# Packing four rows a partition into one slot, with larger store pieces in two half stores, in a transfer-bound SwiGLU kernel

## Chip, cores, metric

One core of a Trainium2 chip. Kernels are compared only within the same rounds. The metric is the device time of one execution in microseconds; lower is better. A "piece" below is one contiguous run of bytes in one partition that a transfer moves; in these traces each piece is one DMA packet.

## The reference

```python
x: float32 [8192, 8192]
a, b = np.split(x, 2, axis=-1)
return a * (b / (1 + np.exp(-b)))        # float32 [8192, 4096]
```

268 MB go in, 134 MB come out; nothing is read twice. The arithmetic is one SiLU and one product for each output element.

## The kernel before

Three slots of 64 KiB in each partition take turns. A slot gets two rows of x a partition (one load of 128 pieces of 64 KiB, 8 MiB). ScalarE overwrites b with SiLU(b), VectorE writes the product over the first half of the slot, and a store of 128 pieces of 32 KiB (4 MiB) sends it out. Loads are issued by SyncE (SP), stores by ScalarE's queue, so they are in two DMA queues (q1 and q10 in the profile).

```python
R = 2; BUFS = 3
xv = x.tensor.reshape([N // R, R * M]).ap()          # one partition line: 2 rows, 64 KiB
ov = out.tensor.reshape([N // R, R * half]).ap()     # one partition line: 2 rows, 32 KiB
...
def swiglu(i, k, c0=0, cw=half):
    xt = tiles[i]
    b = xt[:, k * M + half + c0 : k * M + half + c0 + cw]
    nc.scalar.activation(out=b, in_=b, func=_SILU)
    nc.vector.tensor_mul(out=xt[:, k * half + c0 : ...], in0=xt[:, k * M + c0 : ...], in1=b)
...
for i in range(BUFS):
    load(i)
for i in range(last):
    for k in range(R):
        swiglu(i, k)
    ...
    store(i)
    nxt = i + BUFS
    if nxt < last:
        load(nxt)            # waits until the store of the same slot has landed
    ...                      # the last tile is loaded and stored in smaller parts
```

Of the kernel before, what the change touches and what calls it, by code (L numbers as in the profile page):

```python
# [1 line left out]

# [4 lines left out]

_SILU = mybir.ActivationFunctionType.Silu


@with_exitstack
def kernel(
    ctx: ExitStack,
    tc: tile.TileContext,
    x: bass.AP,
    out: bass.AP,
):




    nc = tc.nc
    N, M = x.shape
    half = M // 2
    P = nc.NUM_PARTITIONS
    R = 2
    BUFS = 3

    xv = x.tensor.reshape([N // R, R * M]).ap()  # L30
    ov = out.tensor.reshape([N // R, R * half]).ap()
    ntiles = N // (P * R)
    last = ntiles - 1

    pool = ctx.enter_context(tc.tile_pool(name="sbuf", bufs=BUFS))
    ctx.enter_context(tc.manual_schedule())
    tiles = {}

    def load(i, rows=None):
        if i not in tiles:  # L40
            tiles[i] = pool.tile([P, R * M], x.dtype, name="xt")
        lo, hi = (0, R) if rows is None else rows
        nc.sync.dma_start(  # L43
            out=tiles[i][:, lo * M : hi * M], in_=xv[i * P : (i + 1) * P, lo * M : hi * M]
        )

    def swiglu(i, k, c0=0, cw=half):
        xt = tiles[i]
        b = xt[:, k * M + half + c0 : k * M + half + c0 + cw]
        nc.scalar.activation(out=b, in_=b, func=_SILU)  # L50
        nc.vector.tensor_mul(  # L51
            out=xt[:, k * half + c0 : k * half + c0 + cw],
            in0=xt[:, k * M + c0 : k * M + c0 + cw],
            in1=b,
        )

    def store(i, c0=0, cw=R * half):
        (nc.scalar if i < last - 1 else nc.sync).dma_start(
            out=ov[i * P : (i + 1) * P, c0 : c0 + cw], in_=tiles[i][:, c0 : c0 + cw]
        )  # L60

    for i in range(BUFS):
        load(i)
    for i in range(last):
        for k in range(R):
            swiglu(i, k)
        if i == last - 1:
            swiglu(last, 0)
        store(i)
        nxt = i + BUFS  # L70
        if nxt < last:
            load(nxt)
        elif nxt == last:
            load(last, (0, 1))
            load(last, (1, 2))

    store(last, 0, half)
    for c0 in range(0, half, half // 2):
        swiglu(last, 1, c0, half // 2)
    store(last, half, half)  # L80


# [1 line left out]
_INS = ['x']  # L84
_OUTS = [((8192, 4096), 'float32')]


# [23 lines left out]
```

## Time and profile before

| | before |
|---|---|
| median, 3 runs before the prediction | 936.1 us (935.9 to 936.24) |
| span of the profiled execution | 934.8 us |
| VectorE, ScalarE busy | 283.3 us, 229.4 us |
| load queue q1, store queue q10, share of the 16 DMA engines | 68.6%, 31.2% |
| bytes moved | 402.65 MB (read 268.44, written 134.22) |

The two queue shares add up to practically all the time of the 16 DMA engines; that is the reading on which everything else stands. The prediction below shows the lines. One view is the order of instructions in the steady part (start, duration, engine and line, what it does; the bracket tells the idle time before it and what ended that):

```profile
398.13 8.95 DVE L51 TENSOR_TENSOR xt<-xt 128x4096 f32<-128x4096 f32 x2 [20.02 <-ACT xt L50]
407.12 0.34 ACTq L58 DMA_DIRECT2D out_dram<-xt  x1
417.89 29.40 SPq L43 DMA_DIRECT2D xt<-in_x_dram  x2
423.51 7.12 ACT L50 ACTIVATE xt<-xt 128x4096 f32<-128x4096 f32 x2 [21.90 <-DMA xt<-in_x_dram]
427.15 8.95 DVE L51 TENSOR_TENSOR xt<-xt 128x4096 f32<-128x4096 f32 x2 [20.07 <-ACT xt L50]
436.14 0.34 ACTq L58 DMA_DIRECT2D out_dram<-xt  x1
```

A store is issued every 29.0 us (407.12, 436.14), and VectorE idles 20 us of them. A store needs 39.7 us to land and a load 34.5, both longer than that distance, so a store is always queued, and so is a load. In the steady part neither queue runs empty.

### The profile page before, as it was taken

How to read it: one execution, taken by the hardware profiler on the slowest of the kernel's cores; microseconds unless marked ns; L12 is line 12 of the kernel's file. 1: busy time of each engine (PE TensorE's matmuls, PEld its weight loads, DVE VectorE, ACT ScalarE, POOL GpSimd, SP SyncE). 2: the span in 40 equal slices, each digit the busy share in tenths (PEclk: the TensorE clock that was granted, in tenths of full speed). 3: DMA queues.
4: the chain of work that ended last, by engine and by line, in shares of the span. 5: the costliest groups of instructions: out<-in, count | busy, mean ns of one | idle time of the engine just before them, and what ended most of it. 6: DMA issues, size and time to landing. Idle time of an engine off the chain costs nothing.

```text
span 934.8 us, 367 instructions
## 1 busy us (share of the span) xinstructions
DVE 283.3 (30%) x65; ACT 229.4 (25%) x66; POOL 0.2 (0%) x4
## 2 busy tenths in 40 slices
DVE  0333312333123331133321333213332133331242
ACT  0223320233302333113331133311333203332041
POOL 0000000000000000000000000000000000000000
DMA  9999999999999999999999999999999999999998
GB/s 404 400 445 430 430 439 433 428 435 443 428 430 439 429 442 432 435 426 453 419 430 452 411 452 423 428 447 425 433 433 453 414 443 429 426 447 428 425 437 376
DMA packets 9506, 402.67 MB, mean 431 GB/s; under 512 B 1056, under 2 KB 1056, under 8 KB 1056
## 3 DMA queue, kind: packets, MB, share of 16 engines
q1 hardware_dynamic: 5184, 276.83, 68.6%
q10 hardware_dynamic: 4320, 125.83, 31.2%
q14 instruction: 2, 0.02, 0.0%
HBM read 268.44 MB, written 134.22 MB: 431 GB/s over the span
## 4 chain that ended last, share of the span: by engine, by line
DMA 84%; DVE 10%; ACT 4%; DVEq 0%; issue 0%; SPq 0%; ACTq 0%
DMA out_dram<-xt 42%; DMA xt<-in_x_dram 42%; DVE xt L51 10%; ACT xt L50 4%; DVEq L106 0%; SPq L43 0%; ACTq L50 0%; DVEq L51 0%
## 5 line engine op out<-in xcount | busy, mean ns | idle before, releaser
L51 DVE TENSOR_TENSOR xt<-xt 128x4096 f32<-128x4096 f32 (+1 forms) x65 | 283.3, 4359 | 637.7 <-ACT xt L50 634.5
L50 ACT ACTIVATE xt<-xt 128x4096 f32<-128x4096 f32 (+1 forms) x65 | 228.1, 3556 | 688.1 <-DMA xt<-in_x_dram 688.1
L50 ACT ACT_TABLE_LOAD x1 | 1.3, 1283 | 0.7 <-PEq L95 0.7
L95 POOL MEMSET const-bfloat16-1.0<- 128x1 bf16 x1 | 0.1, 103 | 0.0
L95 POOL MEMSET const-uint8-127<- 128x1 uint8 x1 | 0.1, 102 | 0.0
L95 POOL MEMSET const-float32-0.0<- 128x1 f32 x1 | 0.1, 100 | 0.2 <-issue 0.2
L95 POOL MEMSET const-float32-1.0<- 128x1 f32 x1 | 0.1, 99 | 0.0
## 6 DMA issues: line engine op xcount, KB each, us to landing
out_dram<-xt ACTq DMA_DIRECT2D x30, 4096.0 KB, 39.7
xt<-in_x_dram SPq DMA_DIRECT2D x2, 4096.0 KB, 27.1
out_dram<-xt SPq DMA_DIRECT2D x1, 4096.0 KB, 23.6
out_dram<-xt SPq DMA_DIRECT2D x2, 2048.0 KB, 14.5
xt<-in_x_dram SPq DMA_DIRECT2D x31, 34.5
```

The source lines that it names most:

```text
L50: nc.scalar.activation(out=b, in_=b, func=_SILU)
L51: nc.vector.tensor_mul(out=xt[:, k * half + c0 : k * half + c0 + cw], in0=xt[:, k * M + c0 : k * M + c0 + cw], in1=b,)
L95: nc = _bacc.Bacc("TRN2", target_bir_lowering=False, num_devices=1)
```

## The change

Its intent: the store's pieces should be 64 KiB too. For that, four rows a partition form a group. Two rows are loaded into a "pack" slot, the other two into an "extra" slot; all four products are written into the pack slot, which is then 64 KiB of finished output. There are two pack slots and one extra slot, so SBUF holds the same 192 KiB a partition. The store goes out in two halves, even and odd partitions, and the next load of the extra slot is made to wait for the first half ("behind"), although the slot is free as soon as VectorE has read it.

```diff
-    R = 2
-    BUFS = 3
+    ngroups = N // (4 * P) - 1
...
+    extra = pool.tile([P, 2 * M], x.dtype, name="extra")
+    packs = [pool.tile([P, 2 * M], x.dtype, name=f"pack{s}") for s in range(2)]
...
+    load_pack(0)
+    load_extra(0)
+    load_pack(1)
+    for g in range(ngroups):
+        pack = packs[g % 2]
+        for k in range(2):
+            swiglu(pack, k, pack, k)
+        for k in range(2):
+            swiglu(extra, k, pack, 2 + k)
+        rows = o4[g * P : (g + 1) * P, :]
+        first = nc.scalar.dma_start(out=rows[0:P:2, :], in_=pack[0:P:2, :])
+        nc.scalar.dma_start(out=rows[1:P:2, :], in_=pack[1:P:2, :])
+        load_extra(g + 1, behind=first)
+        if g + 2 <= ngroups:
+            load_pack(g + 2)
```

(cut: the loads' addresses, and the last 256 x 2 rows, which go through the same half loads and the same three stores from SP as before)

More of the change, by code (lines that the diff above doesn't have):

```diff
@@ L26 @@
     P = nc.NUM_PARTITIONS
-    R = 2
-    BUFS = 3
-    xv = x.tensor.reshape([N // R, R * M]).ap()
-    ov = out.tensor.reshape([N // R, R * half]).ap()
-    ntiles = N // (P * R)
-    last = ntiles - 1
-    pool = ctx.enter_context(tc.tile_pool(name="sbuf", bufs=BUFS))
-    ctx.enter_context(tc.manual_schedule())
-    tiles = {}
-    def load(i, rows=None):
-        if i not in tiles:
-            tiles[i] = pool.tile([P, R * M], x.dtype, name="xt")
-        lo, hi = (0, R) if rows is None else rows
-        nc.sync.dma_start(
-            out=tiles[i][:, lo * M : hi * M], in_=xv[i * P : (i + 1) * P, lo * M : hi * M]
-        )
@@ L47, in swiglu @@
-    def swiglu(i, k, c0=0, cw=half):
-        xt = tiles[i]
-        b = xt[:, k * M + half + c0 : k * M + half + c0 + cw]
+    ngroups = N // (4 * P) - 1
+    sync_dep = mybir.DependencyInfo(mybir.DependencyClass.Sync, mybir.DependencyReason.DATA)
+    x4 = x.tensor.reshape([N // 4, 4 * M]).ap()
+    o4 = out.tensor.reshape([N // 4, 4 * half]).ap()
+    x2 = x.tensor.reshape([N // 2, 2 * M]).ap()
+    o2 = out.tensor.reshape([N // 2, 2 * half]).ap()
+    pool = ctx.enter_context(tc.tile_pool(name="sbuf", bufs=1))
@@ L50, in swiglu @@
+    ctx.enter_context(tc.manual_schedule())
+    extra = pool.tile([P, 2 * M], x.dtype, name="extra")
+    packs = [pool.tile([P, 2 * M], x.dtype, name=f"pack{s}") for s in range(2)]
+    def swiglu(src, k, dst, d, c0=0, cw=half):
+        b = src[:, k * M + half + c0 : k * M + half + c0 + cw]
         nc.scalar.activation(out=b, in_=b, func=_SILU)
         nc.vector.tensor_mul(
-            out=xt[:, k * half + c0 : k * half + c0 + cw],
-            in0=xt[:, k * M + c0 : k * M + c0 + cw],
+            out=dst[:, d * half + c0 : d * half + c0 + cw],
+            in0=src[:, k * M + c0 : k * M + c0 + cw],
@@ L54, in swiglu @@
             in1=b,
         )
-    def store(i, c0=0, cw=R * half):
-        (nc.scalar if i < last - 1 else nc.sync).dma_start(
-            out=ov[i * P : (i + 1) * P, c0 : c0 + cw], in_=tiles[i][:, c0 : c0 + cw]
-        )
-    for i in range(BUFS):
-        load(i)
-    for i in range(last):
-        for k in range(R):
-            swiglu(i, k)
-        if i == last - 1:
-            swiglu(last, 0)
-        store(i)
-        nxt = i + BUFS
-        if nxt < last:
-            load(nxt)
-        elif nxt == last:
-            load(last, (0, 1))
-            load(last, (1, 2))
@@ L77, with load_pack, load_extra @@
-    store(last, 0, half)
+    def load_pack(g):
+        if g < ngroups:
+            src = x4[g * P : (g + 1) * P, : 2 * M]
+        else:
+            src = x2[2 * ngroups * P : (2 * ngroups + 1) * P, :]
+        nc.sync.dma_start(out=packs[g % 2], in_=src)
+    def load_extra(g, behind=None):
+        if g < ngroups:
+            insts = [nc.sync.dma_start(out=extra, in_=x4[g * P : (g + 1) * P, 2 * M :])]
+        else:
+            r0 = (2 * ngroups + 1) * P
+            insts = [
+                nc.sync.dma_start(
+                    out=extra[:, k * M : (k + 1) * M], in_=x2[r0 : r0 + P, k * M : (k + 1) * M]
+                )
+                for k in range(2)
+            ]
+        if behind is not None:
+            tc.add_manual_dep(
+                insts[0].ins, behind.ins.name, sync_dep, reason="half of the store goes first"
+            )
@@ L78 @@
+    pack = packs[ngroups % 2]
+    r0 = 2 * ngroups * P
+    for k in range(2):
+        swiglu(pack, k, pack, k)
+    swiglu(extra, 0, extra, 0)
+    nc.sync.dma_start(out=o2[r0 : r0 + P, :], in_=pack[:, :M])
+    r0 += P
+    nc.sync.dma_start(out=o2[r0 : r0 + P, :half], in_=extra[:, :half])
     for c0 in range(0, half, half // 2):
-        swiglu(last, 1, c0, half // 2)
-    store(last, half, half)
+        swiglu(extra, 1, extra, 1, c0, half // 2)
+    nc.sync.dma_start(out=o2[r0 : r0 + P, half:], in_=extra[:, half:M])
```

## The prediction

> **What bounds the kernel now.** I read the page's first two parts first, to see whether an engine or the transfers are full; then the queues, to count packets; then the windows and the chain, to see whether transfers ever wait for compute.
>
> ```profile
> DVE 283.3 (30%) x65; ACT 229.4 (25%) x66; POOL 0.2 (0%) x4
> ...
> DMA  9999999999999999999999999999999999999998
> ...
> q1 hardware_dynamic: 5184, 276.83, 68.6%
> q10 hardware_dynamic: 4320, 125.83, 31.2%
> ...
> HBM read 268.44 MB, written 134.22 MB: 431 GB/s over the span
> ```
>
> No compute engine is busy for a third of the span; the 16 DMA engines are at 9 tenths or more in 39 of 40 slices. The two queues' shares add up to 99.8% of all engine time (68.6 + 31.2). The reader should see that there is almost nothing to hide better: no byte goes away in this change, so only time per byte, or the 0.2%, can shrink. The windows say the same for the steady part and for the two ends:
>
> ```profile
> 0.00:46.00 46.00, 8.85 (x2) 8.40 (x3) 0.20 (x4) 1.00 0.98 407
> ...
> 59.00:146.00 87.00, 26.48 (x7) 21.37 (x6) 0.00 (x0) 1.00 1.00 434
> 146.00:233.00 87.00, 26.54 (x7) 21.37 (x6) 0.00 (x0) 1.00 1.00 434
> ...
> 900.00:935.00 35.00, 9.51 (x4) 7.33 (x3) 0.00 (x0) 1.00 0.91 393
> ```
>
> The last two columns are the DMA share and GB/s. In the middle the share is 1.00 at 434 GB/s; only the start and the last microseconds are below. The chain of what ended last looks different at first sight:
>
> ```profile
> DMA 84%; DVE 10%; ACT 4%; DVEq 0%; issue 0%; SPq 0%; ACTq 0%
> DMA out_dram<-xt 42%; DMA xt<-in_x_dram 42%; DVE xt L51 10%; ACT xt L50 4%; DVEq L106 0%; SPq L43 0%; ACTq L50 0%; DVEq L51 0%
> ```
>
> It puts 14% on ACT and DVE, because a slot's own cycle is load, compute, store. While one slot computes, the other two keep both queues full, so those 14% are not a gain to be had.
>
> I also read the trace's single packet records. Every data packet is one contiguous piece of one partition, and its duration depends on size alone: 16 KiB 0.611 us, 32 KiB 1.213 us, 64 KiB 2.418 us (medians; in the steady part nearly all equal them), and a completion packet 0.009 us. A straight line through these is 0.602 us per 16 KiB plus about 0.009 us a packet. Summed and divided by 16 engines they give 932.5 us; the first packet starts at 1.7 us and the last ends at 933.6 us. **Work of the DMA engines is the time.**
>
> [...] 65,536 B in 2.418 us is 27.1 GB/s an engine, 433.7 for 16, and the windows show 434. [...] where both queues have work, each 64 KiB load packet is followed by one 32 KiB store packet. [...]
>
> **The change part by part.**
>
> *Store pieces.* Now 30 stores on ACT's queue move 128 pieces of 32 KiB: 8 an engine, 240 in all, 240 x 1.213 = 291.1 us of each engine. After, 15 groups with two halves of 64 pieces of 64 KiB: 4 an engine, 30 x 4 x 2.418 = 290.2 us. Gain **1.0 us**. This is the whole direct saving: a piece costs 0.009 us beyond its bytes, and 120 pieces an engine go away.
>
> *Loads.* 31 full loads and two half loads before and after, with the same piece sizes: 0 us. Completion packets: 33 + 33 transfers before, 33 + 33 after: 0 us.
>
> *Compute.* The same 65 ACTIVATE (3.60 us) and 65 products (4.43 us), only another destination slot: 0 us, and beside transfers in any case.
>
> *Last tiles.* The same half loads, the same three stores from SP (one of 4 MiB, two of 2 MiB): 0 us. The final load still lands some 20 us of transfers before the end, with stores queued, so compute stays covered.
>
> *New waits.* The order has to be played through, since 3 slots now hold a group and a half. Per group an engine has 16 load pieces (38.7 us) and 8 store pieces (19.3 us): 58.0 us. Let the stores be issued at T with R us of the next pack load still to come. Pieces alternate one to one and are equally long, so the pack load ends at T + 2R, the first half store (9.7 us) at T + R + 9.7. The extra load may then start; I allow 1.2 us for the store's completion (last packet's end to the end of the span, 933.6 to 934.8) and 1.3 us for issue (first load: issued 0.73, first packet 1.74). During these 2.5 us the second half store runs alone; its remaining 7.2 us share with the extra load and take 14.3. The extra load then runs its last 12.1 us alone, with the next pack load queued behind it. It lands 1.3 us later, and its two rows need 3.6 + 2 x 4.43 us and small gaps, 12.7 in all, during which the pack load runs. So R = 19.3 - 14.0 = 5.3 us, and the group takes 5.3 + 9.7 + 2.5 + 14.3 + 12.1 + 14.0 = 58 us, which is the work. **No engine idles**: the margin is 7.2 us at the first wait (second half still to send) and 5.3 us at the second (pack load still in the queue). Waiting for the first half thus costs nothing, if half stores run at full rate.
>
> Sum: 936.1 - 1.0 = 935.1 us. Start and end losses (first packet 1.7 us, last receipt 1.2 us, slow first packets) stay.
>
> **Rivals.**
>
> [...] Full collision adds 290 us (1225 us); a quarter of the store time colliding adds 73 us (1008 us). It is the only way that I see to a large loss.
>
> *B, a new bubble.* If the completion of a half store took 10 us instead of 1.2, the extra load would start late and both queues would be empty: 15 x some 2 us, 965 us. Against: in the last part of the trace receipt is 1.2 us, and the margins are 5 us and more.
>
> [...]
>
> *D, faster than the count.* Equal pieces in both queues change how reads and writes mix. Against: load pieces take 2.418 us alone (first 30 us) and beside stores alike; there is nothing to win from another mix. [...]
>
> **Range and chances.** With no collision and no bubble the count is tight: 933 to 937 us. I give this nearly 80%. A gets most of the rest, and spreads from 950 to over 1100 us. The range 932 to 960 takes the first case and a mild form of B or C. Faster by over 2%: 0.01; within 2%: 0.79; slower: 0.20.
>
> **What would show it.** Right: 15 x 2 stores of 64 pieces on ACT's queue, 30 x (64 + 16) = 2400 packets in q10 where 4320 were, at about 31.1% of the span; q1 unchanged in packets; DMA share 1.00 and 434 GB/s in windows of 58 us; half stores 10 to 30 us from issue to landing. Wrong by A: q10's share well above 31%, store packets over 2.418 us, GB/s below 420 in the steady part with the DMA share still near 1. Wrong by B: DMA share below 0.97 in the steady windows with packets at 2.418 us. Wrong by C: load packets longer as well.

The text names two rivals. A: the engines that move a half store of 64 partitions slow each other, so that a store packet takes up to 4.8 us in place of 2.4. That doubling was the author's guess (no transfer in the trace of before had 64 partitions); its 290 and 73 us are estimates from it and from the 290.2 us that the stores take. C: the doubled pitch of the rows slows packets by 1%, also a guess. Two readings that the prediction gives without a count: of the 2308 load packets of 64 KiB between 200 and 800 us that are followed by a data packet, 2303 are followed by one of a store, and of the 3683 between 50 and 900 us, 3666 lie within 1 ns of 2.418 us.

## The result, and the profile after

936.78 us median (936.38 to 937.82, 6 runs) against 936.29 us (935.9 to 937.33, 6 runs) of the kernel before in the same rounds. The ratio is 1.0005, interval 0.9992 to 1.0018: the same. (All ratios are the mean time of one kernel's fast runs over the mean of the other's of the same rounds, so not quite the ratio of the medians.)

The page of the changed kernel, engines, DMA share by slice, queues and the chain of what ended last:

```profile
DVE 281.9 (30%) x65; ACT 229.4 (25%) x66; POOL 0.2 (0%) x4
...
DMA  9999999999999999999999999999999999999998
...
q1 hardware_dynamic: 5184, 276.83, 68.6%
q10 hardware_dynamic: 2400, 125.83, 31.1%
...
HBM read 268.44 MB, written 134.22 MB: 431 GB/s over the span
...
DMA 77%; DVE 14%; ACT 6%; issue 1%; DVEq 0%; SPq 0%; ACTq 0%
```

The store queue has 2400 packets where it had 4320, and its share of engine time went from 31.2% to 31.1%. Half the data packets (1920 in place of 3840), practically the same time: to this resolution a packet's time is its bytes. The windows (us, VectorE and ScalarE busy, GpSimd, clock, DMA share, GB/s):

```profile
0.00:46.00 46.00, 9.31 (x3) 12.51 (x5) 0.20 (x4) 1.00 0.98 416
...
116.00:174.00 58.00, 17.61 (x4) 14.24 (x4) 0.00 (x0) 1.00 1.00 434
174.00:232.00 58.00, 17.61 (x4) 14.24 (x4) 0.00 (x0) 1.00 1.01 434
...
900.00:935.00 35.00, 8.92 (x3) 7.33 (x3) 0.00 (x0) 1.00 0.91 390
```

434 GB/s at full share in the steady part, as before. The order of one group:

```profile
404.39 0.48 ACTq L86 DMA_DIRECT2D out_dram<-pack  x1
404.90 5.21 ACTq L87 DMA_DIRECT2D out_dram<-pack  x1
416.13 7.12 ACT L44 ACTIVATE pack<-pack 128x4096 f32<-128x4096 f32 x2 [17.06 <-DMA pack<-in_x_dram]
419.78 8.95 DVE L45 TENSOR_TENSOR pack<-pack 128x4096 f32<-128x4096 f32 x2 [15.42 <-ACT pack L44]
420.96 0.33 SPq L62 DMA_DIRECT2D extra<-in_x_dram  x1
437.78 0.33 SPq L57 DMA_DIRECT2D pack<-in_x_dram  x1
449.91 7.12 ACT L44 ACTIVATE extra<-extra 128x4096 f32<-128x4096 f32 x2 [26.66 <-DMA extra<-in_x_dram]
453.56 8.76 DVE L45 TENSOR_TENSOR pack<-extra 128x4096 f32<-128x4096 f32 x2 [24.83 <-ACT extra L44]
462.35 0.48 ACTq L86 DMA_DIRECT2D out_dram<-pack  x1
```

The stores go out at T = 404.39, the extra load at T + 16.6, the pack load at T + 33.4, and the next stores at T + 58.0. The prediction's play-through gives 16.2, 33.0 and 58. The chain of what ended last shifts some of its shares from transfers to engines (DMA 84% to 77%, VectorE 10% to 14%, ScalarE 4% to 6%), and the time didn't move. That fits the prediction's reading of the chain: its engine shares aren't time to be gained while another slot's transfers fill the same microseconds.

The trace's packet records (not a view of the page: every packet with its queue, start, duration and size) say where each microsecond is. I use two sums over them, each divided by 16 engines: **stretch**, the time of data packets beyond the usual duration of their size (2.418 us for 64 KiB, 1.213 for 32, 0.611 for 16), and **idle**, the time from the first packet's start to the last packet's end less all packet time. Idle can be slightly negative, because the records of one engine's successive packets overlap by some nanoseconds. A **completion packet** is one of 4 bytes that each engine sends when its share of a transfer is done; the 66 transfers of either kernel left 16 of them each. The records don't name the engine; where the text speaks of one engine, its packets are put together by one ending where the next begins.

| run | median, us | before in its rounds | ratio (95%) | stretch, us | idle, us |
|---|---|---|---|---|---|
| before | 936.29 | | | 2.2 | -0.6 |
| the change | 936.78 | 936.29 | 1.0005 (0.9992 to 1.0018) | 2.6 | -0.3 |
| after_again | 936.61 | 936.32 | 1.0003 (0.9991 to 1.0016) | 2.8 | -0.2 |
| store_blocks | 1160.40 | 936.33 | 1.2387 (1.2366 to 1.2408) | 221.6 | 4.8 |
| load_blocks | 1240.48 | 936.33 | 1.3246 (1.3222 to 1.3270) | 306.4 | -0.6 |
| quarter_pieces | 944.21 | 936.33 | 1.0080 (1.0065 to 1.0095) | | |
| whole_wait | 991.57 | 936.32 | 1.0591 (1.0577 to 1.0606) | 29.7 | 27.8 |
| whole_free | 966.93 | 936.32 | 1.0341 (1.0321 to 1.0362) | 28.0 | 4.8 |
| halves_free | 1010.34 | 936.32 | 1.0791 (1.0776 to 1.0805) | 50.1 | 26.2 |
| quarters_third | 940.48 | 936.11 | 1.0052 (1.0037 to 1.0067) | 7.7 | 0.2 |
| quarters_first | 983.69 | 936.11 | 1.0504 (1.0486 to 1.0521) | 31.0 | 19.3 |
| halves_free_32k | 960.45 | 936.21 | 1.0266 (1.0245 to 1.0286) | 23.5 | 2.4 |
| quarters_first_32k | 940.68 | 936.21 | 1.0046 (1.0030 to 1.0063) | 5.8 | 0.1 |

All outputs are right. The two columns explain the times: for halves_free, 50.1 + 26.2 less the 2.2 - 0.6 of the kernel before is 74.7 us, and it was 74.0 us slower than that kernel. The columns are those of the profiled run, which for quarters_third was its slowest (942.15 us). quarter_pieces has none, since its 8 KiB pieces have no usual duration above. At a threshold of 2%, quarter_pieces, quarters_third and quarters_first_32k count as the same as before, but their intervals lie clear of 1.

### The profile page after: what moved, and what is told of

Read it like the earlier page. It is cut to its first block, busy times and chain, and to the rows that moved or that the text cites. A ratio compares the mean times of both kernels' runs of the same rounds, so it can differ in the third digit from the quotient of the medians.

```text
span 934.6 us, 367 instructions
## 1 busy us (share of the span) xinstructions
DVE 281.9 (30%) x65; ACT 229.4 (25%) x66; POOL 0.2 (0%) x4
## 3 DMA queue, kind: packets, MB, share of 16 engines
q1 hardware_dynamic: 5184, 276.83, 68.6%
q10 hardware_dynamic: 2400, 125.83, 31.1%
## 4 chain that ended last, share of the span: by engine, by line
DMA 77%; DVE 14%; ACT 6%; issue 1%; DVEq 0%; SPq 0%; ACTq 0%
DMA extra<-in_x_dram 51%; DMA out_dram<-pack 27%; DVE pack L45 13%; ACT extra L44 6%; DVE extra L45 0%; DVEq L128 0%; SPq L62 0%; SPq L57 0%; SPq L66 0%; ACTq L44 0%
## 5 line engine op out<-in xcount | busy, mean ns | idle before, releaser
L45 DVE TENSOR_TENSOR pack<-extra 128x4096 f32<-128x4096 f32 x30 | 131.4, 4422 | 359.4 <-ACT extra L44 359.4
L45 DVE TENSOR_TENSOR pack<-pack 128x4096 f32<-128x4096 f32 x32 | 141.6, 4425 | 260.2 <-ACT pack L44 258.5
L44 ACT ACTIVATE extra<-extra 128x4096 f32<-128x4096 f32 (+1 forms) x33 | 114.2, 3505 | 410.5 <-DMA extra<-in_x_dram 410.5
L44 ACT ACTIVATE pack<-pack 128x4096 f32<-128x4096 f32 x32 | 114.0, 3608 | 277.5 <-DMA pack<-in_x_dram 277.5
L45 DVE TENSOR_TENSOR extra<-extra 128x2048 f32<-128x2048 f32 (+1 forms) x3 | 8.9, 3000 | 19.3 <-ACT extra L44 19.3
```

Source lines behind the costliest of these rows:

```text
L45: nc.vector.tensor_mul(out=dst[:, d * half + c0 : d * half + c0 + cw], in0=src[:, k * M + c0 : k * M + c0 + cw], in1=b,)
```

## Experiments

The prediction was right, so the questions are why nothing was lost, where the expected 1 us went, and which parts of the change carry weight. Theory: the DMA engines are full before and after (932.4 and 931.9 us of packet time); the split into even and odd partitions keeps the store packets at 2.418 us, where blocks of 64 neighbouring partitions would not; and the wait for the first half keeps both queues from running empty. Rivals: neither matters; or they matter and for other reasons.

### after_again: is there a microsecond?

No edit; the changed kernel in five more rounds.

> The changed kernel once more, unedited, with more rounds, to size a difference of less than 1 us. Theory of the prediction (each store piece costs about 0.009 us beyond its bytes, 120 fewer per engine): 1.0 us faster than before, ratio 0.999. Theory formed after the result: the records of successive packets overlap by some nanoseconds (waves of load packets start 2.414 us apart but are recorded as 2.418), and the group period fell by only 0.02 us (58.04 to 58.02 us), so the true saving is about 0.3 us, ratio 0.9997, not to be told from 1.

Measured: ratio 1.0003, 0.9991 to 1.0016, again not below 1. The gain of 1.0 us (ratio 0.999) lies just outside both intervals; the 0.9997 of the theory formed after the result lies inside. The records do show the saving in the stores, 291.1 to 290.2 us, but the stretch of load packets took back 0.4 us, and the records overlap less. One stretch of 0.44 us is at 192 to 197 us in both profiles of the changed kernel and not in that of before; I don't know its cause.

### quarter_pieces: what does a packet cost?

The kernel before with the same bytes and waits in four times as many packets:

```diff
-        nc.sync.dma_start(
-            out=tiles[i][:, lo * M : hi * M], in_=xv[i * P : (i + 1) * P, lo * M : hi * M]
-        )
+        for c in range(lo * M, hi * M, M // 2):
+            nc.sync.dma_start(
+                out=tiles[i][:, c : c + M // 2], in_=xv[i * P : (i + 1) * P, c : c + M // 2]
+            )
...
+        step = cw // 4 if i < last - 1 else cw
+        for c in range(c0, c0 + cw, step):     # the store in `step` columns at a time
```

> The kernel before with every load piece cut from 64 to 16 KiB and every steady store piece from 32 to 8 KiB, same ratio of the two, same slots and waits: 1480 more data packets and 185 more completion packets per engine. Theory of the prediction (0.009 us a packet): 1480 x 0.0087 + 185 x 0.009 = 14.5 us more, 951 us. Theory formed after the result (packet records overlap; the true cost of a piece is 2 to 5 ns): 4 to 9 us more, 940 to 945 us. If pieces cost nothing: 936 us.

Measured: 944.21 against 936.33, 7.9 us more for 1480 data and 185 completion packets on each engine: 4.7 ns a packet. The recorded durations sum to 13.1 us more (945.5 against 932.4); successive packets overlap by the rest. If every packet costs the same, the 120 pieces that the change saves are worth about 120 x 4.7 ns = 0.6 us (an estimate), not 1.0, and 0.4 us came back as stretch. The kernel before agrees: on one engine a 32 KiB packet is followed by the next after 1.209 us, a 64 KiB packet after 2.414, so two of the one cost 0.004 us more than one of the other.

### store_blocks and load_blocks: does it matter which 64 partitions?

In store_blocks the halves are partitions 0 to 63 and 64 to 127; in load_blocks the stores stay even and odd, and each extra load of a group is cut at partition 64, both parts behind the first half store. The theory under test is that a block of 64 neighbouring partitions slows the packets, to as much as double their time.

```diff
-        first = nc.scalar.dma_start(out=rows[0:P:2, :], in_=pack[0:P:2, :])
-        nc.scalar.dma_start(out=rows[1:P:2, :], in_=pack[1:P:2, :])
+        first = nc.scalar.dma_start(out=rows[: P // 2, :], in_=pack[: P // 2, :])
+        nc.scalar.dma_start(out=rows[P // 2 :, :], in_=pack[P // 2 :, :])
```

```diff
-            insts = [nc.sync.dma_start(out=extra, in_=x4[g * P : (g + 1) * P, 2 * M :])]
+            src = x4[g * P : (g + 1) * P, 2 * M :]
+            insts = [
+                nc.sync.dma_start(out=extra[h : h + P // 2, :], in_=src[h : h + P // 2, :])
+                for h in (0, P // 2)
+            ]
```

> The two half stores take partitions 0 to 63 and 64 to 127 instead of even and odd ones; waits as in the changed kernel. [...] store packets go from 2.418 us to as much as 4.8 us where all engines are in step, which adds up to 290 us; 1000 to 1225 us, DMA share near 1, load packets still 2.418. Rival (reads from SBUF don't collide, or the share is spread in another way): 936 us, packets unchanged; then the choice of every second partition had no effect and my rival A was no danger in the first place.

> The stores stay even and odd; the 15 extra loads are cut in two transfers of partitions 0 to 63 and 64 to 127, both behind the first half store. Tests writes into SBUF as store_blocks tests reads. [...] these load packets (120 per engine, 290 us) take up to 4.8 us, 1000 to 1225 us. Rival (only reads collide): 936 us; rival (neither collides): 936 us here and in store_blocks.

Queues of store_blocks (packets, MB, share of the 16 engines) and GB/s in 40 slices of the span:

```profile
GB/s 403 430 269 378 371 285 434 260 382 373 274 434 269 376 378 260 434 290 367 392 253 434 281 364 391 260 434 281 357 394 249 434 294 346 403 240 434 305 311 374
...
q1 hardware_dynamic: 5184, 276.83, 56.9%
q10 hardware_dynamic: 2400, 125.83, 42.5%
```

The same 2400 packets and bytes as in the changed kernel now take 42.5% of a longer span, 492 us of each engine in place of 290. The reader should see the slices: 434 GB/s where only loads run, 240 to 300 where stores take most of the slice. In the records the median store packet takes 4.90 us in place of 2.42. Of the 221.6 us of stretch 201.5 lie in store packets; load packets have the other 20, which the expectation had at zero.

Queues of load_blocks:

```profile
q1 hardware_dynamic: 5424, 276.83, 76.1%
q10 hardware_dynamic: 2400, 125.83, 23.7%
```

Here the load queue takes 76.1% of 1238.5 us, 942 us in place of 641, and the median store packet stays at 2.418 us. Over the 120 packets of an engine's extra loads those 301 us are 2.5 us each, so about 4.9 us a packet (an estimate from the two shares). Both runs show that a block of 64 partitions is slow, for stores out of SBUF and for loads into it, and refute the rivals, which all expected 936 us. What in the hardware makes it slow isn't shown. DMA share stays near 1 (0.99 to 1.02 in three windows of store_blocks, at 319 to 363 GB/s, and 9 tenths or more in 39 of 40 slices of load_blocks): the share counts the time that packets take, whatever they move in it. A cause on the DRAM side was not tested by a run of its own, but is unlikely: the whole store of whole_free writes the same contiguous rows, and the whole extra load reads the same rows at the same pitch, both with a median of 2.418 us. In the changed kernel, with even and odd partitions, no packet showed this (store packets at 2.418 us, stretch of all stores 0.06 us). It isn't so in every order of transfers: halves_free and halves_free_32k below, with the same split, have 5.1 and 7.1 us of stretch in store packets, of open cause. How the 64 partitions were dealt to the engines isn't recorded; all that is shown is that this split kept full rate in the changed kernel and the block split did not.

### whole_wait, whole_free, halves_free: what do the halves and the wait do?

whole_wait: one store of all partitions, extra load behind it. whole_free: one store, extra load free of it. halves_free: two halves, extra load free of them.

```diff
-        first = nc.scalar.dma_start(out=rows[0:P:2, :], in_=pack[0:P:2, :])     # whole_wait, whole_free
-        nc.scalar.dma_start(out=rows[1:P:2, :], in_=pack[1:P:2, :])
+        first = nc.scalar.dma_start(out=rows, in_=pack)
...
-        load_extra(g + 1, behind=first)                                          # whole_free, halves_free
+        load_extra(g + 1)
```

> One whole store, and the extra load waits for all of it. Theory: the pack load ends, the store runs alone to its end, then nothing is queued until its completion is seen and the next load issued: 2.2 to 2.5 us idle for all engines per group, 15 x 2.2 to 2.5 = 33 to 37 us, so 969 to 973 us, with the DMA share in steady windows at about 0.96 and packets still 2.418 us. Rival (transfers are covered whatever the order, because the queues are deep): 936 us.

> One store of 128 pieces of 64 KiB in place of two halves, and the extra load doesn't wait for it. Theory: the halves serve only the wait; without it one whole store does as well, 936 us, same as halves_free to 1 us. Rival (halves give something of their own, for example earlier landing): slower by 1% or more than halves_free.

> The wait of the extra load on the first half store is taken away; the extra load then waits only for the products that read its slot. Played through with the prediction's method: extra load and store share from the start, the store ends 38.7 us after its issue, the next pack load is issued 2.5 us later while the load queue still has 2.8 us of work, so no engine idles: 936 us, same within 1 us, with half stores taking longer to land (around 20 us and 40 us in place of 16.5 and 33) and the pack load issued some 41 us after the stores instead of 33. Rival (the wait is what keeps the queues full): a bubble each group, 15 x 1 to 3 us, 950 to 980 us.

All three were slower than expected, halves_free and whole_free against my theory. The order in whole_wait:

```profile
424.71 0.34 ACTq L86 DMA_DIRECT2D out_dram<-pack  x1
437.36 7.12 ACT L44 ACTIVATE pack<-pack 128x4096 f32<-128x4096 f32 x2 [17.97 <-DMA pack<-in_x_dram]
...
452.27 0.33 SPq L62 DMA_DIRECT2D extra<-in_x_dram  x1
452.64 0.43 SPq L57 DMA_DIRECT2D pack<-in_x_dram  x1
473.95 7.12 ACT L44 ACTIVATE extra<-extra 128x4096 f32<-128x4096 f32 x2 [29.46 <-DMA extra<-in_x_dram]
477.60 8.76 DVE L45 TENSOR_TENSOR pack<-extra 128x4096 f32<-128x4096 f32 x2 [27.63 <-ACT extra L44]
486.39 0.34 ACTq L86 DMA_DIRECT2D out_dram<-pack  x1
```

The group takes 61.7 us in place of 58.0. Nothing is queued between the end of the store and the load issued at 452.27, and the records have a gap (fewer than 8 of 16 engines at work) of 1.7 to 2.0 us there in each of the 15 groups. That much was expected. The other half of the loss was not: after each gap the first load packets take 3.1 us (0.65 us an engine), and when the next store starts, each engine's load packet before it takes 3.6 us (1.2 us). The kernel before has this pattern once, at its start (0.6 us) and at its first store (1.5 us).

The order in halves_free:

```profile
434.58 0.33 SPq L62 DMA_DIRECT2D extra<-in_x_dram  x1
434.59 0.48 ACTq L86 DMA_DIRECT2D out_dram<-pack  x1
435.10 0.63 ACTq L87 DMA_DIRECT2D out_dram<-pack  x1
...
483.29 0.33 SPq L57 DMA_DIRECT2D pack<-in_x_dram  x1
485.69 7.12 ACT L44 ACTIVATE extra<-extra 128x4096 f32<-128x4096 f32 x2 [29.95 <-DMA extra<-in_x_dram]
```

The pack load is issued 48.7 us after the stores, where I expected some 41, and by then the extra load had practically been through: the load queue was empty: gaps of about 1 us and more (0.95 to 4.0) in 11 of the 15 groups. The records show what my play-through had left out. In this group 15 engines end their last store data at 477.3 to 478.7 us, and their completion packets run at 479.7 to 481.1, each 2.41 us later: **a completion packet takes a turn of its own and waits behind one 64 KiB load packet.** The slowest engine is nearly 2 us behind the others (480.5, its completion 482.9), and SP issues 0.4 us after that last one. So time is the wrong unit for the margin; turns are the right one. Where both queues have work they alternate packet by packet (the 2303 of 2308 above), and completion packets are part of that: in the kernel before, each of the 480 completion packets of its store queue came right behind a load packet, 464 of them 2.41 us after the last store data. With the wait taken away the store needs 8 data and 2 completion turns, and the load queue holds about 2 packets of the pack load and 8 of the extra load: nothing is left when the last completion is seen. With one whole store there is one completion turn fewer, and indeed whole_free idles 4.8 us in all and not 26.2. In the changed kernel the extra load comes in when about half of the store is gone, so most of its 8 packets are left. Idle time is the smaller part of what halves_free lost: of its 74 us, some 27 are idle time and 48 stretch, and turns explain only the idle part.

### quarters_third and quarters_first: moving the wait

The store in four quarters of every fourth partition, the extra load behind the third or the first of them.

```diff
+        parts = [
+            nc.scalar.dma_start(out=rows[q:P:4, :], in_=pack[q:P:4, :]) for q in range(4)
+        ]
+        load_extra(g + 1, behind=parts[2])      # quarters_first: parts[0]
```

> The store in four quarters of every fourth partition (32 pieces of 64 KiB each), the extra load behind the third. Theory as corrected by the earlier runs (only a moment with both queues empty costs: about 1.9 us of gap, then about 0.65 us at the restart and 1.2 us at the next store; a completion packet waits its turn behind one load packet, 2.4 us, and engines are up to 3 us apart): when the third quarter is done two store pieces an engine, 4.8 us, are still queued, and a new load needs about 1.4 us from completion to its first packet on an idle engine, so no gap: 936 to 938 us, packets at 2.418 us. Rival (the nearer the wait is to the end of the store, the more is lost): between the changed kernel and the whole-store wait, 950 to 980 us. [...]

> As the other, the extra load behind the first quarter. Corrected theory: the last store data ends about 33 us after the issue, its completion packet 2.4 us later, the slowest engine up to 3 us after that, the next pack load's first packet at about 40 us; the extra load keeps the load queue busy to some 42.7 us. A margin of 0 to 3 us: 936 to 945 us, likelier near 937. Rival (any earlier start of the extra load costs, as it did without the wait): near the whole store without wait, 960 us or more.

quarters_third did nearly what was expected (936 to 938 us): no idle time, 940.5 us, some 4 us over the kernel before, most of it in small stretches of 0.1 to 0.4 us where a store starts (and 0.9 us once). Its store packets, of every fourth partition, 32 at a time, kept their median of 2.418 us. quarters_first missed, at 983.7 us. Its order:

```profile
419.43 8.04 ACTq L87 DMA_DIRECT2D out_dram<-pack  x4
...
433.85 0.33 SPq L62 DMA_DIRECT2D extra<-in_x_dram  x1
...
466.01 0.33 SPq L57 DMA_DIRECT2D pack<-in_x_dram  x1
```

The pack load is issued 46.6 us after the stores; I had allowed 40. I had counted one completion turn, but four quarter stores have four. After the first quarter 6 data and 3 completion packets are left, up to nine turns, against 8 packets of the extra load. So I formed the theory of turns in full and tested it by changing one size.

### halves_free_32k and quarters_first_32k: more turns in the load queue

Both with the extra load as two transfers by columns, so that its pieces are 32 KiB and it has 16 packets an engine. Bytes, slots and waits stay.

```diff
-            insts = [nc.sync.dma_start(out=extra, in_=x4[g * P : (g + 1) * P, 2 * M :])]
+            src = x4[g * P : (g + 1) * P, 2 * M :]
+            insts = [
+                nc.sync.dma_start(out=extra[:, c : c + M], in_=src[:, c : c + M])
+                for c in (0, M)
+            ]
```

> halves_free (no wait of the extra load, 1010 us) with one size changed: the extra load in two transfers by columns, so its pieces are 32 KiB. Theory of turns: queues alternate packet by packet whatever the size, and a completion packet takes a turn like a data packet. In halves_free the store needs 8 + 2 turns and the load queue holds only 2 + 8 packets and a completion, so it runs dry before the store's completion is seen and the next load is issued. With 32 KiB pieces the load queue holds 2 + 16 packets and 2 completions, the store is through after 10 of them and 12 us of load work are still queued: no gap, no stretched packets, 936 to 939 us. Rival (the early start of the extra load costs in itself, by reads beside writes): still 990 us or more.

> quarters_first (extra load behind the first of four quarter stores, 984 us) with the extra load's pieces at 32 KiB. Theory of turns: 6 store pieces and 3 to 4 completion packets, 9 to 10 turns, against 8 load packets there; against 16 here. No gap: 936 to 940 us. Rival (four stores or an early wait cost in themselves): still 970 us or more.

quarters_first went from 983.7 to 940.7 us; its idle time went from 19.3 to 0.1 us and its stretch from 31.0 to 5.8. The time is just above the expected 936 to 940. halves_free went from 1010.3 to 960.5, and so missed its 936 to 939; its idle time went from 26.2 to 2.4 us, as the theory says, but 23.5 us of stretch stayed, about 0.8 us of it at each store's start. Smaller load pieces didn't lower the cost of bytes by themselves (quarter_pieces took 7.9 us more), so the theory of turns is shown for the idle time. What makes packets stretch is not settled: that they stretch only after both queues ran empty, as I thought after whole_wait, is refuted by halves_free_32k, which stretches without a gap. quarters_first_32k, with a similar mix, hardly does.

No variant beat the kernel before. At 932 us of packet time in a span of 935 there was nothing left to find in the order of transfers.

## Why the prediction was right

*What bounds the kernel.* Right. Work of the DMA engines is the time, before (932.4 us of packet records) and after (931.9).

*The store pieces, minus 1.0 us.* The mechanism was there and the size was off. The step took the packet's extra cost of about 0.009 us from the recorded durations. quarter_pieces measured 4.7 ns, which makes it 0.6 us. 0.4 us of stretch came on top, and the medians differ by 0.3 to 0.5 us the other way, which the intervals can't tell from zero.

*Loads, compute, last tiles: 0 us.* Right within 0.4 us (the stretch of loads); the queue q1 has the same 5184 packets and 68.6%, and the engines' busy times differ by 1.4 us at most, off the path.

*The new waits: no engine idles.* Right in its result and close in its times (16.6, 33.4 and 58.0 us), but incomplete as a method. "Waiting for the first half thus costs nothing" holds, and the runs show more: with these sizes of pieces some such wait is needed. Take it away and the kernel loses 74 us (48 of them stretch, whose cause is open); put it at the whole store and it loses 55. The play-through had no completion turns, no spread between engines and no stretch, so it gave halves_free and quarters_first a margin that they didn't have. It was right for the changed kernel because its margin was large enough for the terms left out, which was luck so far as they were not known: when the next pack load was issued, 12.1 us of the extra load were still to land (437.78 and 449.91), a margin that the play-through contains but doesn't list. One sign was put too narrowly as well: "half stores 10 to 30 us" contradicts the 33 us of its own play-through, and the second halves took 32.9.

*Rival A, half stores that collide.* It did not happen: the store packets kept 2.418 us. store_blocks and load_blocks show that the danger was real (4.90 us a store packet in blocks of 64 partitions). Why every second partition avoids it isn't shown, and how the engines got their partitions isn't recorded. The estimate of 290 us for full collision was roughly right: 224 us, and 304 us, which is above it. My fifth of a chance for "slower" went mostly to this; the trace of before held nothing that could have excluded it.

*Rival B, a bubble.* It did not happen; its size was underrated. A gap of about 2 us a group costs 55 us in 15 groups, not 30, since packets stretch as well.

*Rival C, the doubled pitch.* No sign: with the pitch at 128 KiB, the load packets have a median of 2.418 us and q1 keeps its share. *Rival D* didn't happen either: the steady part moves 434 GB/s before and after.

## What to carry to other kernels

When the shares of the DMA queues add up to the whole span, as here (68.6% + 31.2%), larger pieces can win only what a packet costs beyond its bytes: count packets, multiply by a few nanoseconds (4.7 in quarter_pieces), and compare with the noise before rebuilding a pipeline. When a transfer is split by partitions, try every second or fourth partition and check the durations of its packets: both kept the store packets at 2.418 us here (the changed kernel, quarters_third), while blocks of 64 partitions ran at about half rate (4.90 us in store_blocks), with a DMA share near 1. When slots are few, count turns and not microseconds: a load that waited for an event left no gap when its queue held more packets than the other queue had data and completion packets in front of that event (quarters_first_32k: 16 against up to nine, idle 0.1 us; quarters_first: 8 against up to nine, idle 19.3 us). That removes idle time only: halves_free_32k met it and still lost 24 us (stretch 23.5 us, against 2.2 in the kernel before).
